# Three passes of the output projection cut anew (pairs 0-3 | query tiles 0-3 with pairs 4-5 | pairs 6-7 with tiles 4-7), passes that hold other tasks while they wait, and a shorter warm-up

## The chip, the cores and the metric

The kernel runs on one NeuronCore of one Trainium2 chip. The metric is the device time of one execution in microseconds, the median of a few runs. TensorE (PE) does the matrix products into PSUM, VectorE (DVE), ScalarE (ACT) and GpSimd (POOL) the rest of the arithmetic; SyncE (SP) issues most DMAs, ACT some. The instructions of each engine stand in one order, fixed when the program is built, and wait on semaphores for the other engines.

## What is computed

One trunk layer of a decoder for a prompt of 256 tokens and 8 single-token decode sequences (264 columns together): a half-step SwiGLU feed-forward, a mixing block in which half of the heads are sliding-window attention with sinks and half are an RWKV-7 recurrence, an output projection with residual, a second half-step feed-forward and a last normalisation.

```python
x = x + FFN_RES * swiglu(rmsnorm(x, n1), f1g, f1u, f1d)
h = rmsnorm(x, nm)
proj = h @ w_in
...
o_att, k_buf, v_buf = attend(q, k, v, sinks)
o_rwkv, shift, S = rwkv_time_mix(proj[..., ATT_COLS:], shift0, wkv0, mu, w0, w2, a0, a2, g2,
                                 k_k, k_a, r_k, ln_w, ln_b)
mixed = jnp.concatenate([o_att, o_rwkv.astype(o_att.dtype)], axis=-1)
x = x + mixed @ w_out
x = x + FFN_RES * swiglu(rmsnorm(x, n2), f2g, f2u, f2d)
...
y = rmsnorm(x, final_norm)
```

The model width is 2048, the feed-forward width 5504, the weights are float32.

## The kernel before

Activations stand transposed: 16 tiles of 128 features by 264 columns. Every large product is made from two-part operands: a weight tile and an activation are each split into a rounded part `hi` (type fp32r) and a remainder `lo`, and three matmuls of 264 columns (hi·hi, hi·lo, lo·hi) take the place of one. `chunk` (line 116) brings the weights: a DMA on SP's queue of up to four 128x128 blocks into `raw` (six buffers), a cast to `hi` on ACT (line 123), a subtraction to `lo` on DVE (line 124); `hi` and `lo` have four buffers each. `gemm` (line 127) runs the three matmuls per block (line 74 is the helper through which all matmuls go) into a PSUM tile `acc` (three buffers), and calls `step` after each chunk. The other PSUM tiles, `m`, have five buffers.

Three stages follow each other: `first_ffn`, `mixing`, `second_ffn`. In `mixing` the kernel is written as generators. The list `tasks` holds those that are under way, and `tick` (line 78) takes each of them one `yield` further. While the 38 tiles of the input projection are made by `win` (line 367), `tick` is the step of `gemm`, so that after each chunk every task issues its next piece. The tasks are: `prep` and `chain`, the recurrence of a batch of two pairs of heads (`bat[0]` to `bat[3]`, pairs 0-1, 2-3, 4-5, 6-7; the chain solves a triangular system on DVE, writes the result `Xt` to DRAM (`sb`, line 546) and reads it back into `TT` (line 551), both on SP's queue, and ends with a group norm, `gnorm`); `kvtask`; `attend`, the attention of one query tile over the prompt (eight tiles, named `o`); and `dec_attend(p)`, the decode attention of four tiles at once, which writes the last 8 columns of these tiles (line 824). `dec_load(p)` brings the cache for it.

The output projection (line 880 on) sums 16 tiles of `mixed`: entries 0 to 7 are the pairs of the recurrence (tiles `y`), 8 to 15 the query tiles (tiles `o`). It runs in passes, by the table

```python
PASS = [[0,1,2,3,8,9,10,11],[4,5,6,7],[12,13,14,15]]
```

A pass first calls `drain(need(ks))`: it ticks all tasks until the ones that made its inputs have ended. Then `split` (line 871) casts each input to `s` on ACT (line 873) and takes the remainder on POOL for even and on DVE for odd indices, and for each of the 16 outputs one `gemm` over the inputs of the pass follows, again with `tick` as step, and an addition on DVE into the residual (line 890). So the passes have 24, 12 and 12 matmuls an output. The rows of `w_out` are laid out by the same table (line 982).

The order on each engine is not the order of writing alone: the framework schedules the whole recorded program by a model of its timeline, with priority by the place in the program, and raises what stands under `tc.high_priority()` (the weights' chunks, the splits of a pass, the additions into the residual).

At the start of the program stands a warm-up of TensorE: POOL fills the constant tile `C` with ones, DVE casts it into a buffer of the ring `hi`, and 44 matmuls of 512 down to 128 columns run on it (lines 153 to 158), while the first inputs are loaded.

Of the kernel before, what the change touches and what calls it, by code (L numbers as in the profile page):

```python
# [8 lines left out]
F32R = mybir.dt.float32r  # L9
# [4 lines left out]
P = 128  # L14
# [13 lines left out]
CH, NRAW, NHL = 4, 6, 4  # L28
NACC, NM = 3, 5
NS, NO, NY, NH, NT, NLD = 38, 8, 8, 40, 18, 6  # L30
WARM = (512,) * 6 + (384,) * 6 + (264,) * 8 + (256,) * 8 + (192,) * 8 + (128,) * 8
NGM, NKR, NUV, NTT, NBT = 10, 5, 3, 2, 5
NSTEP = 4
DWAIT = (8,8,8,4)
# [2 lines left out]
LKV = 26  # L37
SEQ = [('b', 0), ('b', 1), ('b', 2), ('b', 3), ('kv', 0), ('kv', 1), ('kv', 2), ('kv', 3), ('q', 0), ('q', 1), ('q', 2), ('q', 3), ('q', 4), ('q', 5), ('q', 6), ('q', 7)]
NSO = (12, 13)
PASS = [[0,1,2,3,8,9,10,11],[4,5,6,7],[12,13,14,15]]  # L40

VG1, VGM, VG2, VGF = 0, 16, 32, 48
VMU, VKK, VKA, VA0, VRK, VLW, VLB, VSK, VSD = 64, 90, 98, 106, 114, 122, 130, 138, 154
# [4 lines left out]
def body(tc, I, O):  # L48
# [4 lines left out]
    def uid(s):  # L53
        cnt[0] += 1
        return f"{s}{cnt[0]}"
# [17 lines left out]
    def mm(out, lhsT, rhs, start=True, stop=True, **k):  # L73
        TE.matmul(out, lhsT, rhs, start=start, stop=stop, **k)  # L74

    tasks = []
# [6 lines left out]
    def drain(only, hold=()):  # L83
        while any(g in only for g in tasks):
            tick(hold)

    def spawn(g):
        tasks.append(g)
        return g
# [5 lines left out]
    with ExitStack() as ctx:  # L95
# [54 lines left out]
        G.memset(eps[:, 1:2], 64e-5)  # L150
        act(eps[:, 0:1], eps[:, 0:1], AF.Copy)

        G.memset(C, 1.0)
        wr = wp.tile([P, CH * P], F32R, tag="hi", bufs=NHL, name=uid("hi"))
        V.tensor_copy(wr, C[:, :CH * P])
        warm = mp()
        for n in WARM:
            mm(warm[:, :n], wr[:, :P], wr[:, :n])

        def vc(i):  # L160
            return vec[:, i:i + 1]
# [173 lines left out]
        def mixing_body(mx, n2, n3, XD):  # L335
# [351 lines left out]
            def kvtask(w, p, x):  # L687
                A.dma_start(O[("kp", "vp")[w]][p], x[:, P:NP])
                yield
                tp = mp()  # L690
                TE.transpose(tp[0:8, 256:384], x[:, NP:T], ident)
                if w:
                    for tb in range(2):
                        TE.transpose(tp[:, tb * P:(tb + 1) * P], x[:, tb * P:(tb + 1) * P], ident)
                    Vt[p] = slot((P, 2, P))
                    A.copy(Vt[p], tp[:, :256].rearrange("p (c t) -> p c t", c=2))
                if p == 0:
                    kvn[w] = tmp((8, 256))
                A.copy(kvn[w][:, p * P:(p + 1) * P], tp[0:8, 256:384])
                if p:  # L700
                    A.dma_start(O[("ks", "vs")[w]][:, 127, :], kvn[w])
                    if w:
                        A.dma_start(vnd, kvn[w])
                        while bat[-2] in tasks:
                            yield
                        dec_load(0)

            def softmax(s, mxv, sinks, n):
                nm, sm, es = (ring((P, 2), "st" + x, 6) for x in "abc")
# [51 lines left out]
            vnd = dp.tile([NB, 256], F32, tag="vnd", name="vnd")  # L761
            dk, dv, db, vr, qb = ([None] * 2 for _ in range(5))

            def dec_load(p):
                dk[p], dv[p] = ring((P, NB, P), "uv", NUV), ring((P, NB, P), "uv", NUV)
                dm = ring((P, 3, 256), "bk", 2)
                qb[p], vr[p], db[p] = (dm[:, i] for i in range(3))
                qb[p] = qb[p].rearrange("p (b x) -> p b x", b=NB)
                vr[p] = vr[p].rearrange("p (s x) -> p s x", s=2)
                db[p] = db[p][:, 0:129]  # L770
                SP.dma_start(dk[p], I["kc"][p])
                SP.dma_start(dv[p], I["cw"][p])
                SP.dma_start(db[p], I["bd"][p])
                G.memset(qb[p], 0.0)
                src = vnd.rearrange("(s g) d -> g s d", s=2)
                for g in range(4):
                    SP.dma_start(vr[p][g * 32:g * 32 + 32],
                                 bc(src[g:g + 1, :, p * P:(p + 1) * P], (32, 2, P)))

            def dec_attend(p, qs):  # L780
                for i, q in enumerate(qs):
                    for h in range(2):
                        G.tensor_copy(qb[p][HALF[h], :, h * 4 + i], q[HALF[h], NP:T])
                yield
                yield
                sps = mp()
                for b in range(NB):
                    g, x = b % 4 * 32, b // 4 * 129
                    mm(sps[g:g + 32, x:x + P], qb[p][:, b], dk[p][:, b])
                for b in range(NB):  # L790
                    g, x = b % 4 * 32, b // 4 * 129 + P
                    mm(sps[g:g + 32, x:x + 1], qb[p][:, b], kT[p][:, NP + b:NP + b + 1])
                dm = ring((P, 768), "bk", 2)
                s = dm[:, 0:258].rearrange("p (s x) -> p s x", s=2)
                pt = dm[:, 258:514].rearrange("p (s x) -> p s x", s=2)
                od = dm[:, 514:546].rearrange("p (i b) -> p i b", i=4)
                mxv = ring((P, 2), "mxv", 6)
                for j in range(2):
                    V.tensor_tensor_reduce(out=s[:, j], in0=sps[:, j * 129:j * 129 + 129], in1=db[p], op0=ALU.add,
                                           op1=ALU.max, scale=1.0, scalar=vc(VSD + p), accum_out=mxv[:, j:j + 1])  # L800
                softmax([s[:, 0], s[:, 1]], mxv, vc(VSD + p), 2)
                yield
                yield
                tp = mp()
                for j in range(2):
                    TE.transpose(tp[:, j * P:(j + 1) * P], s[:, j, 0:P], ident)
                A.copy(pt, tp[:, 0:2 * P].rearrange("p (s x) -> p s x", s=2))
                yield
                op = mp()
                for b in range(NB):  # L810
                    g, j = b % 4 * 32, b // 4
                    mm(op[g:g + 32, j * P:(j + 1) * P], pt[:, j, g:g + 32], dv[p][:, b])
                oa = tmp((P, 2, P))
                for j in range(2):
                    stt(oa[:, j], vr[p][:, j], s[:, j, P:P + 1], op[:, j * P:(j + 1) * P], ALU.mult, ALU.add)
                yield
                tq = mp()
                for j in range(2):
                    TE.transpose(tq[:, j * P:(j + 1) * P], oa[:, j], ident)
                tv = tq[:, :2 * P].rearrange("p (b x) -> p x b", b=NB)  # L820
                for h in range(2):
                    A.copy(od[HALF[h]], tv[HALF[h], h * 4:h * 4 + 4, :])
                for i, q in enumerate(qs):
                    G.tensor_copy(q[:, NP:T], od[:, i])
                if p == 0:
                    while bat[-1] in tasks:
                        yield
                    dec_load(1)

            shifted(0, la)  # L830
            act(tw[0:64, :], la[0:64, :], AF.Tanh)
# [3 lines left out]
            for kind, i in SEQ:  # L835
# [18 lines left out]
                else:  # L854
# [6 lines left out]
                    if i % 4 == 3:  # L861
                        p = i // 4
                        d = spawn(dec_attend(p, qs[4 * p:]))
                        for a in att[4 * p:]:
                            a.append(d)
            n2.xs = None
            xr = [slot() for _ in range(KD)]
            for o in range(KD):
# [10 lines left out]

            k0 = 0  # L880
            for pi, ks in enumerate(PASS):
                drain(need(ks))
                with tc.high_priority():
                    for k in ks:
                        split(k)
# [158 lines left out]
```

## Time and profile before

| what | value |
| --- | --- |
| time, median of 3 runs | 2030.97 us (2028.06 to 2032.6) |
| the profiled execution's own time | 2028.85 us |
| its span, first to last instruction | 2027.1 us, mean granted clock of TensorE 0.993 |
| TensorE matmul busy | 1990.2 us, 98% of the span |
| DVE, ACT, POOL busy | 1329.2, 1039.3, 243.0 us |
| data moved | 347.58 MB read, 10.22 MB written, 177 GB/s over the span |

A row of a timeline gives the start in us from the span's start, the duration in us, engine, line, operation, the tile written and the tiles read, how often it occurs there, and in brackets the idle time of the engine ahead of it with the instruction that ended it. A row of a windows table gives a stretch of time and in it the busy time and number of instructions of each engine, the granted clock as a share of full speed, the share of the DMA engines' time and GB/s. Matmuls overlap, so the time of one is read from the distance of starts or from a count in a window, not from its own duration. A matmul of plain float32 stands in the trace as two.

### The profile page before, as it was taken

Reading aid. Unit: us, or ns where it says so; the run is one execution under the profiler, and the core shown is the slowest. Engines: PE = TensorE matmul, PEld = TensorE weight load, DVE = VectorE, ACT = ScalarE, POOL = GpSimd, SP = SyncE. Lnnn points to the kernel's source line nnn. Section 1 sums busy time; section 2 is a strip of 40 time slices with the busy share of each in tenths; the row PEclk is TensorE's granted clock in tenths of the full one; section 3 lists DMA queues with packets and bytes.
Section 4 is the critical chain, followed back from the end, with each engine's and each line's share of the span. In section 5 each row is a group of like instructions: output and inputs, shape, how many; then the busy total and the mean of one; then the engine's idle time right before and its main releaser. Section 6 shows DMA issues by size and latency. Waiting matters only on the chain.

```text
span 2027.1 us, 45546 instructions
## 1 busy us (share of the span) xinstructions
PE 1990.2 (98%) x17142; PEld 1954.5 (96%) x17142; DVE 1329.2 (66%) x2659; ACT 1039.3 (51%) x2038; POOL 243.0 (12%) x343
## 2 busy tenths in 40 slices
PE   9999999999999999999897999999999999999998
PEld 9999999999999999999896799999999999999998
DVE  5865555655556577678777767775666666666665
ACT  5644444444444467665454654554444444444445
POOL 0401001010110122121110000120101101010012
PEclk9999999999999999999998999999999999999999
DMA  6566565655556566554455245565666565656654
GB/s 228 177 187 197 183 193 188 186 184 176 186 170 192 181 206 206 149 160 123 139 152 168 86 135 181 172 185 178 191 182 195 182 190 188 189 192 181 195 181 145
DMA packets 226493, 358.72 MB, mean 177 GB/s; under 512 B 42312, under 2 KB 79328, under 8 KB 226272
## 3 DMA queue, kind: packets, MB, share of 16 engines
q1 hardware_dynamic: 219808, 347.28, 55.0%
q10 hardware_dynamic: 6464, 8.54, 1.3%
q8 instruction: 134, 2.20, 0.4%
q14 instruction: 87, 0.71, 0.1%
HBM read 347.58 MB, written 10.22 MB: 177 GB/s over the span
## 4 chain that ended last, share of the span: by engine, by line
PE 90%; DVE 4%; DMA 3%; SPq 1%; issue 1%; ACT 1%; POOL 0%; DVEq 0%; ACTq 0%; POOLq 0%
PE acc L74 82%; PE m L74 7%; DVE lo L58 1%; DMA raw<-in_win 1%; DMA TT<-sb 1%; DMA sb<-Xt 0%; DVE t L680 0%; DVE st L58 0%; SPq L530 0%; DVE Xt L58 0%; DVE y L58 0%; ACT L68 0%; DMA Xt<-sa 0%; DMA raw<-in_wout 0%; ACT t L68 0%
## 5 line engine op out<-in xcount | busy, mean ns | idle before, releaser
L58 DVE TENSOR_TENSOR lo<-raw,hi 128x512 fp32r<-128x512 f32 (+1 forms) x1288 | 870.3, 679 | 539.1 <-ACT hi L123 515.5
L123 ACT CAST hi<-raw 128x512 fp32r<-128x512 f32 (+1 forms) x1288 | 777.0, 607 | 855.1 <-PE acc L74 776.3
L74 PE MATMUL acc<-s,hi 128*128 128x264 f32 x5940 | 1105.6, 286 | 7.4 <-ACT s L873 7.4
L74 PEld LDWEIGHTS acc<-s,hi 128*128 128x128 f32 x5940 | 922.7, 188 | 12.9 <-ACT s L873 8.2
L74 PE MATMUL acc<-s,lo 128*128 128x264 f32 x2970 | 846.8, 286 | 4.1 <-DVE lo L58 4.0
L74 PEld LDWEIGHTS acc<-s,lo 128*128 128x128 f32 x2970 | 559.0, 188 | 6.7 <-DVE lo L58 5.1
L74 PE MATMUL acc<-t,hi 128*128 128x264 f32 x2752 | 503.0, 284 | 0.0
L74 PEld LDWEIGHTS acc<-t,hi 128*128 128x128 f32 x2752 | 426.5, 188 | 0.0
L74 PE MATMUL acc<-t,lo 128*128 128x264 f32 x1376 | 389.1, 285 | 0.0
L58 POOL TENSOR_TENSOR t<-t,t 128x264 f32<-128x264 f32 (+1 forms) x148 | 151.1, 1021 | 1149.0 <-ACT hi L123 790.1
L74 PEld LDWEIGHTS acc<-t,lo 128*128 128x128 f32 x1376 | 258.5, 188 | 0.1
L74 PE MATMUL acc<-y,hi 128*128 128x264 f32 x648 | 124.1, 285 | 0.0
L74 PEld LDWEIGHTS acc<-y,hi 128*128 128x128 f32 x648 | 101.1, 188 | 0.2
L74 PE MATMUL acc<-y,lo 128*128 128x264 f32 x324 | 92.0, 284 | 0.0
L58 DVE TENSOR_TENSOR t<-acc,t 128x264 f32<-128x264 f32 x156 | 67.3, 432 | 35.8 <-PE acc L74 35.6
L58 POOL TENSOR_TENSOR o<-o,o 128x264 f32<-128x264 f32 x43 | 36.5, 850 | 229.8 <-ACT o L68 224.9
L74 PE MATMUL acc<-o,hi 128*128 128x264 f32 x324 | 62.6, 283 | 0.0
L74 PEld LDWEIGHTS acc<-y,lo 128*128 128x128 f32 x324 | 60.9, 188 | 0.0
L61 DVE SCALAR_TENSOR_TENSOR s<-acc,s 128x264 f32<-128x264 f32 x96 | 40.5, 427 | 16.0 <-PE acc L74 15.5
L74 PEld LDWEIGHTS acc<-o,hi 128*128 128x128 f32 x324 | 49.8, 188 | 0.0
L74 PE MATMUL m<-s,hi 128*128 128x264 f32 x260 | 47.8, 284 | 0.0
L61 DVE SCALAR_TENSOR_TENSOR x<-acc,x 128x264 f32<-128x264 f32 x96 | 40.4, 426 | 10.0 <-PE acc L74 9.6
(236 smaller groups left out, 1300.9 us busy)
## 6 DMA issues: line engine op xcount, KB each, us to landing
raw<-in_gu SPq DMA_DIRECT2D x688, 256.0 KB, 3.3
raw<-in_dn SPq DMA_DIRECT2D x224, 256.0 KB, 2.8
raw<-in_win SPq DMA_DIRECT2D x152, 256.0 KB, 3.5
raw<-in_dn SPq DMA_DIRECT2D x160, 192.0 KB, 2.8
raw<-in_wout SPq DMA_DIRECT2D x64, 256.0 KB, 3.2
xsp<-x ACTq DMA_DIRECT2D x16, 132.0 KB, 3.7
s<-xsp SPq DMA_DIRECT2D x16, 132.0 KB, 3.4
ld<-in_sT SPq DMA_DIRECT2D x16, 128.0 KB, 3.3
```

Of the source, the lines that this page charges most:

```text
L58: return e.tensor_tensor(out=out, in0=a, in1=b, op=op)
L61: return V.scalar_tensor_tensor(out=out, in0=a, scalar=s, in1=b, op0=op0, op1=op1)
L74: TE.matmul(out, lhsT, rhs, start=start, stop=stop, **k)
L123: A.copy(hi[:, :w], raw[:, :w])
```

## The change

Four things are edited.

1. The table `PASS` becomes `[[0,1,2,3],[8,9,10,11,4,5],[6,7,12,13,14,15]]`: 12, 18 and 18 matmuls an output. The chunks of a pass of six inputs are of four and of two blocks, so the projection has 80 chunks where it had 64, of the same bytes in all, and 80 ticks.
2. A pass that waits takes on only the tasks it needs: `drain(now, [g for g in tasks if g not in now])`.
3. `dec_load` becomes a task of its own that waits for the tasks whose buffers it takes over; `dec_attend` waits until its tiles are there. Before, `kvtask` and `dec_attend(0)` waited in its place.
4. The warm-up is 14 plain float32 matmuls of 128 columns on the tile `ones`; the fill of `C` and the cast are gone.

```diff
-WARM = (512,) * 6 + (384,) * 6 + (264,) * 8 + (256,) * 8 + (192,) * 8 + (128,) * 8
+NWARM = 14
...
-PASS = [[0,1,2,3,8,9,10,11],[4,5,6,7],[12,13,14,15]]
+PASS = [[0,1,2,3],[8,9,10,11,4,5],[6,7,12,13,14,15]]
...
-        G.memset(C, 1.0)
-        wr = wp.tile([P, CH * P], F32R, tag="hi", bufs=NHL, name=uid("hi"))
-        V.tensor_copy(wr, C[:, :CH * P])
         warm = mp()
-        for n in WARM:
-            mm(warm[:, :n], wr[:, :P], wr[:, :n])
+        for _ in range(NWARM):
+            mm(warm[:, :P], ones, ones)
...
                     if w:
                         A.dma_start(vnd, kvn[w])
-                        while bat[-2] in tasks:
-                            yield
-                        dec_load(0)
+                        spawn(dec_load(0, [bat[-2]]))
...
-            def dec_load(p):
+            def dec_load(p, after):
+                while any(g in tasks for g in after):
+                    yield
                 dk[p], dv[p] = ring((P, NB, P), "uv", NUV), ring((P, NB, P), "uv", NUV)
...
             def dec_attend(p, qs):
+                while dk[p] is None:
+                    yield
                 for i, q in enumerate(qs):
...
                     G.tensor_copy(q[:, NP:T], od[:, i])
-                if p == 0:
-                    while bat[-1] in tasks:
-                        yield
-                    dec_load(1)
...
                         for a in att[4 * p:]:
                             a.append(d)
+                        if p == 0:
+                            spawn(dec_load(1, [bat[-1], d]))
...
             for pi, ks in enumerate(PASS):
-                drain(need(ks))
+                now = need(ks)
+                drain(now, [g for g in tasks if g not in now])
```

**How the instructions stand, first place: TensorE after the last matmul of the input projection.** `m<-s,o` are attention scores, `m<-sgl,ld` the gate of pairs 4-5, `m<-C,t` transposes of softmax results; `acc<-s,...` right behind them are the first matmuls of the output projection. Before:

```order
L74 MATMUL acc_16335<-s_10584,lo_16450 128x264
L74 MATMUL m_15235<-s_14460,o_15157 128x256
L74 MATMUL m_15235<-s_14460,o_15157 128x128
L74 MATMUL m_15274<-sgl,ld_15133 128x264
L74 MATMUL m_15278<-sgl,ld_15135 128x264
L74 MATMUL acc_16538<-s_16506,hi_16540 128x264
L74 MATMUL acc_16618<-s_16506,hi_16620 128x264
L745 MATMUL m_15384<-C,t_15241 128x128
```

And now:

```order
L74 MATMUL acc_16302<-s_10551,lo_16417 128x264
L74 MATMUL m_15202<-s_14427,o_15124 128x256
L74 MATMUL m_15202<-s_14427,o_15124 128x128
L74 MATMUL m_15241<-sgl,ld_15100 128x264
L74 MATMUL m_15245<-sgl,ld_15102 128x264
L74 MATMUL acc_16489<-s_16473,hi_16491 128x264
L74 MATMUL acc_16521<-s_16473,hi_16523 128x264
L74 MATMUL acc_16571<-s_16473,hi_16573 128x264
L74 MATMUL acc_16489<-s_16474,hi_16491 128x264
L74 MATMUL acc_16489<-s_16473,lo_16492 128x264
```

Up to the second-solve products of pairs 6-7 (`m<-TT,zs`) 24 projection matmuls stood before, and 119 stand now; from there to the first product of the decode attention of tiles 0-3 (`m<-uv,bk`) 12 and 61; from there to the first matmul on a query tile none and 12. The attention and recurrence matmuls between them are the same.

**ScalarE at the same place.** `L123 CAST` are weight chunks, `L68 ACTIVATE t,stb` the exponentials of the softmax of query tile 4, `L873 CAST` (now `L870`) the splits of the first pass. Before:

```order
L68 ACTIVATE t_15143<-m_15217,eps 128x264
L123 CAST hi_16694<-raw_16693 128x512
L68 ACT_TABLE_LOAD
L68 ACTIVATE t_15240,stb_15246<-t_15240,sta_15245 128x256
L68 ACTIVATE t_15241,stb_15246<-t_15241,sta_15245 128x128
L68 ACTIVATE stc_15247<-sta_15245,vec 128x2
L68 ACTIVATE t_15292,stb_15298<-t_15292,sta_15297 128x256
L68 ACTIVATE t_15293,stb_15298<-t_15293,sta_15297 128x128
L68 ACTIVATE stc_15299<-sta_15297,vec 128x2
L873 CAST s_16506<-y_12725 128x264
L873 CAST s_16510<-y_12726 128x264
```

And now:

```order
L68 ACTIVATE t_15110<-m_15184,eps 128x264
L123 CAST hi_16649<-raw_16648 128x512
L870 CAST s_16473<-y_12692 128x264
L870 CAST s_16477<-y_12693 128x264
L870 CAST s_16481<-y_13753 128x264
L870 CAST s_16485<-y_13754 128x264
L68 ACT_TABLE_LOAD
L68 ACTIVATE t_15207,stb_15213<-t_15207,sta_15212 128x256
L68 ACTIVATE t_15208,stb_15213<-t_15208,sta_15212 128x128
```

The four splits stood behind both softmax halves of that tile and stand ahead of them now.

**Second place: VectorE where the read-back of the triangular solve of pairs 6-7 is used** (`TT<-TT,C`). `s<-acc,s` is the addition into the residual that frees a bank `acc`, `L736 ISA` (now `L731`) the softmax's maximum. Before, right behind the gate operations:

```order
L736 ISA t_15293,mxv_15294<-m_15235,ld_15192,vec 128x128
L736 ISA mxv_15294 128x1
L58 TENSOR_TENSOR y_14838<-m_15141,t_15143 128x264
L58 TENSOR_TENSOR TT_14729<-TT_14729,C 32x8x32
L65 TENSOR_SCALAR sta_15245<-mxv_15242 128x2
L58 TENSOR_TENSOR TT_14729<-TT_14729,C 32x8x32
```

And now, with the last step of the solve (`Xt`), which stood 16 rows ahead of that place, at its head:

```order
L58 TENSOR_TENSOR Xt_14687<-Xt_14687,st_15252 128x8
L710 RECIPROCAL stb_15213<-stb_15213 128x2
L58 TENSOR_TENSOR stb_15265<-stb_15265,stc_15266 128x2
L65 TENSOR_SCALAR t_15207<-t_15207,stb_15213 128x256
L65 TENSOR_SCALAR t_15208<-t_15208,stb_15213 128x128
```

```order
L731 ISA t_15366,mxv_15367<-m_15359,ld_15329,vec 128x128
L731 ISA mxv_15367 128x1
L58 TENSOR_TENSOR TT_14696<-TT_14696,C 32x8x32 x2
L745 COPY t_15404<-m_15399 128x128
L731 ISA t_15407,mxv_15409<-m_15360,ld_15331,vec 128x256
L731 ISA mxv_15409 128x1
L731 ISA t_15408,mxv_15409<-m_15360,ld_15331,vec 128x128
L731 ISA mxv_15409 128x1
L58 TENSOR_TENSOR s_16444<-acc_16647,s_16444 128x264
```

The solve ends later on DVE, its read-back is used later, and the addition for the fourth output of the first pass stands behind it.

**Third place: TensorE ahead of the first matmul on a query tile.** `m<-uv,bk` and `m<-C,bk` belong to the decode attention, `m<-y,C` and `m<-t,C` to the norm of pairs 6-7. Before:

```order
L74 MATMUL m_15927<-uv_15330,bk_15332 32x128 x8
L74 MATMUL m_15927<-s_14460,bk_15332 32x1 x8
L74 MATMUL m_15987<-y_15617,C 128x264
L74 MATMUL m_15991<-y_15618,C 128x264
L74 MATMUL m_15995<-t_15844,s_14815 64x256
L74 MATMUL m_15995<-t_15907,s_14815 64x256
L74 MATMUL m_15995<-t_15845,s_14815 64x128
L74 MATMUL m_15995<-t_15908,s_14815 64x128
L806 MATMUL m_16022<-C,bk_15944 128x128
```

And now, the last three of the twelve matmuls of the pass's last output being shown:

```order
L74 MATMUL acc_16940<-s_16485,hi_16942 128x264
L74 MATMUL acc_16940<-s_16486,hi_16942 128x264
L74 MATMUL acc_16940<-s_16485,lo_16943 128x264
L74 MATMUL m_15954<-y_15584,C 128x264
L74 MATMUL m_15958<-y_15585,C 128x264
L74 MATMUL m_15962<-t_15811,s_14782 64x256
L74 MATMUL m_15962<-t_15874,s_14782 64x256
L74 MATMUL m_15962<-t_15812,s_14782 64x128
L74 MATMUL m_15962<-t_15875,s_14782 64x128
L805 MATMUL m_15989<-C,bk_15911 128x128
```

Twelve projection matmuls came in between the decode attention's first product and the norm; from the norm on the rows are those of before, up to the first matmul on a query tile.

## The prediction

> **What bounds the kernel now.** I read the page first, then the busy times by stretches, then the timeline where TensorE is not full.
>
> ```profile
> PE 1990.2 (98%) x17142; PEld 1954.5 (96%) x17142; DVE 1329.2 (66%) x2659; ACT 1039.3 (51%) x2038; POOL 243.0 (12%) x343
> PE 90%; DVE 4%; DMA 3%; SPq 1%; issue 1%; ACT 1%; POOL 0%; DVEq 0%; ACTq 0%; POOLq 0%
> L74 PE MATMUL acc<-s,hi 128*128 128x264 f32 x5940 | 1105.6, 286 | 7.4 <-ACT s L873 7.4
> ...
> 1050.00:1100.00 50.00, 48.19 (x583) 43.68 (x582) 38.58 (x123) 23.81 (x53) 2.86 (x7) 1.00 0.61 172
> 1100.00:1150.00 50.00, 36.69 (x437) 28.60 (x436) 36.40 (x138) 25.91 (x86) 3.65 (x11) 0.82 0.37 107
> 1150.00:1200.00 50.00, 50.00 (x393) 42.45 (x393) 35.20 (x119) 28.24 (x86) 3.93 (x11) 0.98 0.38 113
> 1200.00:1250.00 50.00, 50.00 (x414) 50.00 (x413) 38.91 (x72) 25.01 (x44) 2.23 (x4) 1.00 0.52 178
> ```
>
> TensorE sets the end. The fifty us from 1100 are the exception: 36.7 us busy at a clock of 0.82. That is the wait of the first output pass, which the table edits. The last row gives the price of a projection matmul, which all counts below use: 50 us / 414 = 0.1208 us.
>
> The hole in front, engine by engine (PE, ACT, DVE, SP):
>
> ```profile
> 1097.16 0.92 PE L74 MATMUL m<-s,o 64*128 64x256 f32 x4
> 1099.47 0.71 PE L74 MATMUL m<-sgl,ld 128*128 128x264 f32 x2 [0.75 <-DVE mxv L736]
> 1107.59 0.81 PE L74 MATMUL acc<-s,hi 128*128 128x264 f32 x2 [7.41 <-ACT s L873]
> 1109.52 0.47 PE L745 MATMUL m<-C,t 128*128 128x128 f32 x1 [1.12 <-DVE t L65]
> ...
> 1097.15 0.62 ACT L123 CAST hi<-raw 128x512 fp32r<-128x512 f32 x1 [1.51 <-PE acc L74]
> 1103.94 0.51 ACT L68 ACTIVATE t<-t,sta 128x256 f32<-128x256 f32 x1 [4.87 <-DVE sta L65]
> 1107.14 1.33 ACT L873 CAST s<-y 128x264 fp32r<-128x264 f32 x4
> ...
> 1093.79 0.17 DVE L58 TENSOR_TENSOR Xt<-Xt,st 128x8 f32<-128x8 f32 x1
> 1101.28 0.43 DVE L58 TENSOR_TENSOR y<-m,t 128x264 f32<-128x264 f32 x1
> 1103.41 0.41 DVE L58 TENSOR_TENSOR TT<-TT,C 32x256 f32<-32x256 f32 x1 [1.69 <-DMA TT<-sb]
> 1104.38 0.49 DVE L61 SCALAR_TENSOR_TENSOR y<-y,vec,t 128x264 f32<-128x264 f32 x1
> ...
> 1094.82 3.56 SPq L546 DMA_DIRECT2D sb<-Xt  x4
> ```
>
> DVE waits for `TT`, behind it stand the maxima for the softmax, behind these ACT's exponentials, behind these the casts of the splits: TensorE loses 7.41 us. From the solve's end (1093.79) to `TT` (1103.41) pass 9.6 us of DRAM round trip.
>
> The second hole, and the clock:
>
> ```profile
> 1120.13 0.69 PE L74 MATMUL m<-TT,zs 32*32 32x32 f32 x30
> 1134.83 0.65 PE L74 MATMUL m<-uv,bk 128*32 128x128 f32 x16
> 1140.45 0.33 PE L806 MATMUL m<-C,bk 128*128 128x128 f32 x1 [2.99 <-DVE bk L65]
> 1145.44 1.53 PE L74 MATMUL m<-s,o 64*128 64x256 f32 x4 [1.45 <-DVE t L750]
> 1151.60 0.99 PE L74 MATMUL acc<-s,hi 128*128 128x264 f32 x3
> ...
> 1112.00:1114.00 2.00, 2.00 (x12) 2.00 (x10) 0.93 (x5) 0.96 (x5) 0.00 (x0) 0.50 0.04 11
> 1148.00:1150.00 2.00, 2.00 (x8) 1.38 (x6) 1.34 (x5) 1.24 (x6) 0.77 (x4) 0.50 0.29 76
> ...
> 916.97 0.48 PE L74 MATMUL m<-BT,W 64*64 64x64 f32 x4 [1.96 <-DVE uv L598]
> 917.00:919.00 2.00, 2.00 (x34) 1.88 (x36) 1.86 (x6) 0.32 (x1) 0.00 (x0) 0.50 0.18 58
> 919.00:921.00 2.00, 2.00 (x54) 2.00 (x52) 2.00 (x5) 0.00 (x0) 0.00 (x0) 0.67 0.01 4
> ```
>
> After each hole the granted clock is 0.50. A wait of 1.96 us is enough for it at 917, and the 0.50 lasts there for some 3.4 us (2 us and two thirds of the next two): about 1.7 us lost each time.
>
> **The passes and the held tasks.** The order in the text above gives three landmarks on PE: A, the second-solve products (1120.13); B, the decode attention's first product (1134.83); C, the first matmul on a query tile (1151.60). At C the old program has done 36 of 768 projection matmuls, the new one 192; what follows C needs the same attention work and 156 matmuls less: 156 x 0.1208 = 18.8 us gained, if C came at the same time. C comes later, by what the inserted matmuls take and the waits leave:
>
> - *To A*: 95 matmuls more, 11.5 us, so 1131.6 with the old waits. The splits now stand ahead of the exponentials on ACT and can run at 1097.8, so the 7.41 us wait and the half clock after it go. New waits, walking down the new order: the second input's remainder is on DVE behind the `y` of 1101.28 and four operations of up to 0.49 us, at about 1103.0, while PE has 12 matmuls (1.45 us) from 1100.2 (1099.47 + 0.71): 1.3 us. Then, the late read-back: the solve's last step now stands on DVE behind some ten such operations of the gate and the softmax, about 1105.3 instead of 1093.8; 8.6 us later (from 1094.82, when SP began to write, to 1103.41) `TT` is there, 1113.9. Behind it stands the addition that frees a bank for the seventh output; with the maxima in between it ends at about 1116.2. PE has six outputs (8.7 us) and 3 to 4 us of attention (four scores in 0.92 us) until 1113.9: 2.3 us. The second half of `TT` costs some 2 us more, the transposes 0.3. Sum 5.9, where the old program lost 7.41 + 1.12 + half of the 7.4 us at half clock from 1107.6 to 1115, 12.2 in all. So 6.3 us are won and A is at **1125.3**. Bounds: none of the new waits, 1119.4; all of the old loss in the new places, 1131.6.
> - *A to B*: 14.7 us as before, and 49 matmuls, 5.9: **B 1145.9**. DVE gets 0.69 + 0.43 us for each output more,
>
> ```profile
> L58 DVE TENSOR_TENSOR lo<-raw,hi 128x512 fp32r<-128x512 f32 x66 | 45.5, 693 | 12.5 <-ACT hi L123 8.4 <-issue 0.3
> L58 DVE TENSOR_TENSOR s<-acc,s 128x264 f32<-128x264 f32 x48 | 20.6, 431 | 12.0 <-PE acc L74 11.7
> ```
>
>  below the 1.45 us that PE takes for one, so these hide behind it; without that cover each output would cost up to 1.1 us more.
> - *B to C*: 16.8 us before. Twelve matmuls (1.45 us) go into the wait of 2.99; the addition and one `lo` of the same output (0.8) stand ahead of the decode softmax on DVE: 17.6, **C 1163.5**. The tail itself is not touched, it keeps its waits and half clock (bounds: 3.4 less at full clock, 2 more).
>
> Net: 18.8 - (1163.5 - 1151.6) = **6.9 us won**.
>
> The 16 added chunks carry no bytes and stand under full passes after C: nothing; without cover 16 x 0.69 = 11 us at most. The last pass needs pairs 6-7 and tiles 4-7, which were long there before; the decode result of these tiles goes ahead of 42 matmuls (5.1 us) now, and from its last transpose to its write (PE, POOL)
>
> ```profile
> 1197.66 0.33 PE L819 MATMUL m<-C,t 128*128 128x128 f32 x1
> 1199.63 0.57 POOL L824 COPY o<-bk 128x8 f32<-128x8 f32 x4
> ```
>
>  the trace has 2.5 us: hidden, 0; if the splits queue, up to 4. Holding tasks and `dec_load` as a task move rows by a few places in the input projection: 0, bounds 2 either way.
>
> **The warm-up.**
>
> ```profile
> 1.61 0.43 DVE L155 CAST hi<-C 128x512 fp32r<-128x512 f32 x1 [1.61 <-POOL C L153]
> 2.09 7.91 PE L74 MATMUL m<-hi 128*128 128x512 f32 x44 [2.09 <-DVE hi L155]
> 9.84 0.46 PE L74 MATMUL acc<-s,hi 128*128 128x264 f32 x2
> 7.63 1.64 ACT L123 CAST hi<-raw 128x512 fp32r<-128x512 f32 x3
> 8.27 1.90 DVE L58 TENSOR_TENSOR lo<-raw,hi 128x512 fp32r<-128x512 f32 x3
> ...
> 2016.05 1.36 PE L74 MATMUL m<-o,ones 128*128 128x128 f32 x10
> ```
>
> The old warm-up runs until the first real matmul at 9.84, though the first `hi` is there at 8.25. The new one is 28 half-products (the last row: 0.11 us each at full clock, twice that at half), from about 1 to 4 to 7 us. Real work can start at 8.3, 1.5 earlier, but runs at the pace of DVE's remainders until about 11. Then it is all but level with before, and PE has idled about 2 us and been half idle until then: by the row of 917 one to two stretches of half clock, 1.7 to 3.4 us. I take **1.5 us lost**, bounds 1.5 won and 3 lost.
>
> [...]
>
> **Sum.** 6.9 - 1.5 = 5.4 us less than the profiled execution's span of 2027.1 (own time 2028.85, 2.1 below the median 2030.97): span 2021.7, median 2025.6.
>
> **The rivals.**
>
> - [...] 0.10.
> - *The waits close*: `TT` arrives before it is needed and PE runs through (A at 1119.4, tail at full clock, start 0): 6.9 + 5.9 + 3.4 = 16.2 less, 2014.8. For it: PE has 119 matmuls to lay over it. Against: the order on DVE. 0.10.
> - *The wait only moves*: A at 1131.6. 0.6 won and 1.5 lost: 2031.9. It happens when `TT` is late by 6 us more, for instance because SP's queue, where the weight DMAs and the residual's 16 loads stand, issues the write late. 0.17.
> - [...] 0.15.
> - That the change doesn't do what it says is out: the order shows it.
>
> **How the numbers follow.** The forecast has 0.48; its own range is 2020 to 2030, by the bounds on A and the start. A measurement tells 0.2% (4 us, below 2026.9 or above 2035.0) from no change. Faster: 0.36 of the forecast and both first rivals, 0.56. Same: 0.12 of the forecast and 0.14 of the moved wait, 0.26. Slower: the clock and the rest of the moved wait, 0.18. The range leaves out the lower half of the closed waits and the upper part of the clock's: 2014 to 2037.
>
> **What would show it.** Right: no wait of PE for ACT's splits near 1100; `TT<-TT,C` about ten us later than 1103; A near 1125, C near 1163 with both its waits; the first real matmul near 8.3 with long distances until 12. Wrong: A after 1129, half clock across several stretches there, a new wait ahead of the last pass (the splits of tiles 4-7), or the input projection ending off 1097 by more than the start explains.

## The result, and the profile after

| | before, us | changed, us | ratio, 95% interval |
|---|---|---|---|
| first comparison, 12 and 12 runs | 2028.16 (2025.49 to 2032.60) | 2028.22 (2027.16 to 2029.30) | 0.9997 [0.9988, 1.0006] |
| second comparison, 27 and 11 runs | 2030.71 (2026.74 to 2034.35) | 2026.22 (2023.20 to 2029.32) | 0.9979 [0.9970, 0.9988] |
| profiled execution, own time / span | 2028.85 / 2027.1 | 2027.84 / 2026.1; second: span 2024.3 | |

No measurable difference at first, 0.2% faster in the repetition, in intervals that touch at their bounds: -1.2 to 2.4 us gained by the first, 2.4 to 6.1 by the second. The forecast was 5.4.

The page, the stretches and PE's timeline of the changed kernel (in the stretches: us, then busy us and instructions of PE, PEld, DVE, ACT and POOL, then the granted clock; in the timeline: start, duration, what ran, and in brackets the wait ahead of it and its cause):

```profile
PE 1994.1 (98%) x17126; PEld 1956.0 (97%) x17126; DVE 1324.4 (65%) x2674; ACT 1041.4 (51%) x2054; POOL 240.8 (12%) x342
PE 94%; DVE 2%; DMA 2%; ACT 1%; SPq 1%; issue 1%; ACTq 0%; DVEq 0%
L74 PE MATMUL acc<-s,hi 128*128 128x264 f32 x5940 | 1107.3, 286 | 3.9 <-DVE s L58 1.6
```

```profile
1100.00:1150.00 50.00, 46.51 (x556) 39.85 (x554) 41.42 (x151) 26.92 (x81) 1.44 (x2) 1.00 0.53 161
1150.00:1200.00 50.00, 44.45 (x300) 35.14 (x301) 35.17 (x127) 27.20 (x85) 5.63 (x17) 0.86 0.27 78
1200.00:1250.00 50.00, 50.00 (x414) 48.35 (x414) 33.43 (x80) 28.63 (x67) 2.17 (x6) 1.00 0.50 161
```

```profile
1099.74 1.35 ACT L870 CAST s<-y 128x264 fp32r<-128x264 f32 x4
1101.11 1.28 ACT L68 ACT_TABLE_LOAD   x1
...
1101.64 0.71 PE L74 MATMUL m<-sgl,ld 128*128 128x264 f32 x2 [0.85 <-DVE mxv L731]
1104.92 0.39 PE L74 MATMUL acc<-s,hi 128*128 128x264 f32 x1 [1.03 <-DVE s L58]
1112.55 0.41 DVE L58 TENSOR_TENSOR TT<-TT,C 32x256 f32<-32x256 f32 x1 [0.82 <-DMA TT<-sb]
1119.25 0.49 PE L74 MATMUL acc<-s,hi 128*128 128x264 f32 x2 [0.61 <-DVE s L58]
1124.48 0.69 PE L74 MATMUL m<-TT,zs 32*32 32x32 f32 x32
1144.91 0.53 PE L74 MATMUL m<-uv,bk 128*32 128x128 f32 x12
1152.21 0.33 PE L805 MATMUL m<-C,bk 128*128 128x128 f32 x1 [3.21 <-DVE bk L65]
1157.20 0.66 PE L74 MATMUL m<-s,o 64*128 64x256 f32 x1 [1.45 <-DVE t L745]
1165.08 1.42 PE L74 MATMUL acc<-s,hi 128*128 128x264 f32 x3 [1.24 <-ACT s L870]
```

The 7.4 us wait of the first splits is gone: ACT casts all four `s` at 1099.74, ahead of the exponentials. The fifty us from 1100 are nearly full at full clock; the hole now lies behind B (1144.91), in the fifty us from 1150, which before were full. From 1200 on nothing waits.

Stretch by stretch (from starts of matmuls in the traces; "control" and "again" are second executions of the same rows, e4 and e12 below):

| us | before / control | changed / again | table alone / same rows (e1, e3) | warm-up alone (e2) |
|---|---|---|---|---|
| start to the projection's first matmul | 763.63 / 763.73 | 763.72 / 764.16 | 763.97 / 763.66 | 763.60 |
| input projection | 333.32 / 334.12 | 335.30 / 333.57 | 334.77 / 333.38 | 336.17 |
| its last matmul to the second FFN | 161.37 / 160.75 | 156.65 / 156.20 | 153.55 / 153.79 | 166.10 |
| of this, lost: up to A | 12.8 / 12.3 | 5.1 / 5.6 | 12.4 / 12.7 | 10.8 |
| of this, lost: A to B | -0.3 / -0.3 | -2.0 / -2.0 | -2.0 / -2.0 | 5.4 |
| of this, lost: from B on | 12.9 / 12.9 | 17.7 / 16.7 | 7.2 / 7.2 | 14.0 |
| second FFN, first to last matmul | 755.92 / 755.95 | 757.38 / 757.38 | 756.64 / 756.64 | 755.06 |

"Lost" is the length of a stretch less its matmuls, each at the median distance of its kind from its start to the next one's; idle time and half clock both land there. A is the first product of the second solve; in the kernel before, two of the 32 run at 1118.63, ahead of the other thirty at 1120.13. The first profile's sum, changed less before: 0.1 + 2.0 - 4.7 + 1.5 = -1.1 us, and the spans differ by 1.0.

### The profile page after: what moved, and what is told of

It reads as the page before. It is cut to its first block, busy times and chain, and to the rows that moved or that the text cites. A ratio compares the mean times of both kernels' runs of the same rounds, so it can differ in the third digit from the quotient of the medians.

```text
span 2026.1 us, 45592 instructions
## 1 busy us (share of the span) xinstructions
PE 1994.1 (98%) x17126; PEld 1956.0 (97%) x17126; DVE 1324.4 (65%) x2674; ACT 1041.4 (51%) x2054; POOL 240.8 (12%) x342
## 4 chain that ended last, share of the span: by engine, by line
PE 94%; DVE 2%; DMA 2%; ACT 1%; SPq 1%; issue 1%; ACTq 0%; DVEq 0%
PE acc L74 85%; PE m L74 8%; DVE lo L58 1%; DMA TT<-sb 0%; DMA sb<-Xt 0%; DVE y L58 0%; DMA raw<-in_gu 0%; DMA ld<-in_sT 0%; DVE st L58 0%; SPq L122 0%; DVE Xt L58 0%; ACT t L68 0%; DVE uv L595 0%; DMA Xt<-sa 0%; PE m L495 0%
## 5 line engine op out<-in xcount | busy, mean ns | idle before, releaser
L58 DVE TENSOR_TENSOR lo<-raw,hi 128x512 fp32r<-128x512 f32 (+2 forms) x1304 | 871.8, 673 | 552.5 <-ACT hi L123 526.5
L123 ACT CAST hi<-raw 128x512 fp32r<-128x512 f32 (+2 forms) x1304 | 779.3, 602 | 861.6 <-PE acc L74 776.3
```

What stands on the lines that cost most here:

```text
L58: return e.tensor_tensor(out=out, in0=a, in1=b, op=op)
L123: A.copy(hi[:, :w], raw[:, :w])
```

## The experiments

**One part alone (e1 to e4).** Four kernels between the two:

```diff
 e1: before with
-PASS = [[0,1,2,3,8,9,10,11],[4,5,6,7],[12,13,14,15]]
+PASS = [[0,1,2,3],[8,9,10,11,4,5],[6,7,12,13,14,15]]
 e2: before with
-        for n in WARM:
-            mm(warm[:, :n], wr[:, :P], wr[:, :n])
+        for _ in range(NWARM):
+            mm(warm[:, :P], ones, ones)
 (and without the fill of C and the cast)
 e3: changed, with the old warm-up, its fill and its cast put back
 e4: before with
-                drain(need(ks))
+                now = need(ks)
+                drain(now, [g for g in tasks if g not in now])
 and dec_load as a task
```

> The kernel before with the new table of passes alone (old warm-up, old draining, old place of the decode load). Theory: the whole gain of the passes comes from the table, so the stretch from the end of the input projection to the first matmul of the second FFN is 4.7 us shorter than before, as in the changed kernel, the input projection ends where it did before (within 0.3 us), and the median is 4 to 5 us under the kernel before, about 2023.5. Rival 1: the gain needs the held tasks; then the second-solve products come at about 1131.6 and at most 0.6 us are won, about 2027.6. Rival 2: the second FFN is slower by 1.4 us because of the new passes (other slots or queues in it); then its mean distance of matmuls is 122.0 ns, not 121.75, and the median is about 2025.

Measured: 2023.63 us, ratio 0.9974 [0.9964, 0.9985], 5.1 us under the 2028.71 of before beside it. The passes are 7.8 us shorter, more than expected, and the second FFN's mean distance is 121.88 ns, between theory and rival 2. Rival 1 is out: the gain needs no held task. But it lies elsewhere than in the changed kernel, from B on.

> The kernel before with the new, short warm-up alone. Theory: the 2.07 us that the input projection lost in the changed kernel come from this edit, since it alone changes the order of the rows between 800 and 1100 us; the first real matmul is at 8.3, the first FFN is level with before from about its 100th matmul, the projection ends 2.07 us later, nothing else changes, and the median is about 2 us above the kernel before, 2030.2. Rival 1: the 2.07 us come from the held tasks and the decode load; then this kernel is level with before from 20 us to the end, 2028.2. Rival 2 (the prediction's term): the start itself loses 1.5 us; then the first FFN ends 1.5 us late.

Measured: 2035.18 us, 1.0033 [1.0021, 1.0044]: slower by 6.5. The start is level, against rival 2, and the projection 2.9 us longer; but the larger loss, 4.7 us, is in the passes, where the theory had none.

> The changed kernel with the old warm-up put back. Theory: it has the gain of the passes without the loss in the input projection: 4.7 us from the end of the projection to the second FFN, and no loss ahead, so about 2023.5, better than both kernels, and the same as the new table alone. Rival: the 2.07 us belong to the held tasks; then this kernel ends where the changed kernel does, 2028, and differs from the table alone by 2 us.

Measured: 2023.95 us, 0.9974 [0.9965, 0.9984], as e1; below the changed kernel's 0.9997, while its second interval, from 0.9970 on, overlaps. The traces have it 2.4 to 2.9 us ahead in the passes and 0.7 in the second FFN. Compared row by row, e1 and e3 issue the same instructions in the same order on all five engines.

> The kernel before with the held tasks and the decode load as a task, but the old table of passes and the old warm-up. Theory: with the old table these two edits move no row, so every landmark is within 0.2 us of before and the median 2028.2; the second FFN's mean distance of matmuls then shows how far two executions of the same rows differ. Rival: they are worth something by themselves, a gain or loss of 1 us or more, seen between 1040 and 1155 us.

Measured: 2029.55 us, 1.0002 [0.9993, 1.0011], and again the same rows as before: holding tasks and spawning `dec_load` change nothing, with either table. It is a control: passes within 0.6 us, second FFN within 0.03, projection 0.8 apart.

What moves rows between 800 and 1260 us is thus the table and the warm-up at the start. That holding and spawning move nothing agrees with a scheduler that sorts the rows by a timeline of its own; that the warm-up's length shifts this is seen in e10 and e11, where only the count of its products differs. PE, ACT and the 6 us stretches of the table with the old warm-up (e3):

```profile
1107.37 1.03 PE L74 MATMUL acc<-s,hi 128*128 128x264 f32 x3 [7.09 <-ACT s L873]
...
1154.00:1160.00 6.00, 5.78 (x47) 4.52 (x47) 6.00 (x12) 1.58 (x4) 0.37 (x2) 1.00 0.11 36
1160.00:1166.00 6.00, 3.89 (x25) 2.44 (x22) 4.33 (x20) 4.17 (x12) 3.28 (x13) 1.00 0.58 162
1166.00:1172.00 6.00, 5.83 (x41) 4.74 (x42) 5.41 (x17) 4.93 (x17) 2.31 (x3) 1.00 0.06 21
```

and what PE waited for from 1097 to 1260 in the new warm-up with the old table (e2; total, times, longest):

```profile
PE m L74 <- DVE stb L712: 3.6, 1, 3.6
PE m L74 <- DVE TN L558: 2.3, 1, 2.3
PE acc L74 <- ACT s L870: 2.2, 1, 2.2
```

With the table and the old warm-up the wait in front stays (7.09 for ACT's splits), but 93 of the 192 matmuls of the first pass are left at B, and the clock reads 1.00 through the tail, 1154 to 1172. With the new warm-up the splits come early, 180 are used up by B, and the tail is bare, with the clock at 0.78, 0.50 and 0.58 in the same three stretches. With the new warm-up and the old table the first splits come early too (from 1100.5), but only 36 matmuls stand ready: two new waits just ahead of A (3.6 and 2.3) and one behind B for the splits of the query tiles (2.2).

**Filling the place behind B (e5 to e8).** Pairs 4-5 are ready at 1106 (their last `y`), and can be a pass of their own; and the splits of pairs 0-3 can be issued by a task of their own, ahead of query tile 7 (EARLY is 6):

```diff
 e5: changed, e6: e3, each with
-PASS = [[0,1,2,3],[8,9,10,11,4,5],[6,7,12,13,14,15]]
+PASS = [[0,1,2,3],[4,5],[8,9,10,11],[6,7,12,13,14,15]]
 e7: e3, e8: e6, each with
+            def early():
+                while any(g in tasks for g in bat[:2]):
+                    yield
+                with tc.high_priority():
+                    for k in PASS[0]:
+                        split(k)
...
+                    if i == EARLY:
+                        es = spawn(early())
...
+                if pi == 0:
+                    now = [es]
...
+                if pi:    # the splits of the later passes alone
```

> The changed kernel with a fourth pass: pairs 4-5 (whose y is ready at 1106) as a pass of their own after pairs 0-3, then query tiles 0-3, then pairs 6-7 with tiles 4-7. Theory: the changed kernel closes the hole in front by spending nearly all of its 192 matmuls there (180 are done when the decode attention begins, and 12 are left for the waits behind it), so the waits of 3.2, 1.5 and 1.2 us and the half clock come back behind it; 96 more matmuls (11.6 us) that need no query tile fill that place. Lost time from the decode attention's first product to the second FFN falls from 17.7 us to 8 to 11, the median from 2028.2 to about 2020. Rival: the waits there are latencies of DVE's chain, which the passes' own additions and splits lengthen, so that the end comes no earlier; then within 2 us of the changed kernel.

Measured: 2019.61 us, 0.9953 [0.9940, 0.9965]. Lost from B on 9.1 us, not 17.7; passes 147.6 us. The theory holds. (The changed kernel's ratios to the same kernel before are 0.9997 and 0.9979.)

> The same four passes with the old warm-up, where the hole in front stays (the casts of the first splits stand behind the exponentials on ACT) and 93 matmuls are still left at the decode attention. Theory: the place behind it is already nearly filled there (7.2 us lost), so the 96 matmuls more bring at most 3 us: 2021 to 2024; the front still loses 12 to 13 us. Rival: the additional matmuls are worth as much here as with the new warm-up, 7 us: 2017.

Measured: 2023.87 us, 0.9971 [0.9959, 0.9982], level with e3; 12.8 us lost in front, 7.1 from B on. So 96 more matmuls are worth 9 us of the passes where the place is bare and nothing where it is filled.

> The three passes of the change with the old warm-up, and the splits of pairs 0-3 issued as soon as their pairs are done, two query tiles earlier, so that their casts stand ahead of the exponentials on ACT; the input projection keeps its order. Theory: matmuls that need no query tile are a fixed amount, 192; by its order this kernel has them all done when the decode attention begins, so what the front gains (lost time 12.7 to about 4 us) the place behind loses (7.2 to about 17), and the time is 2022 to 2026, level with the old warm-up without it (2023.9). Rival: the two holes are independent; then it gains 8 us and is at 2016.

Measured: 2019.17 us, 0.9952 [0.9940, 0.9965]: 4.7 us under e6 beside it (which is level with e3), between theory and rival. Not all of it is the passes: in the profiled executions they are 2.6 us shorter than in e6 and the second FFN 2.0 shorter (755.13, not 757.17), which neither has a term for, while the projection is 2.0 longer. In front 3.6 us are lost, as expected; from B on 12.7, not 17, with no matmul of the first pass left. Its tail has the first two waits of the changed kernel's, not the third, and more clock: 0.85 and 0.87 in the stretches from 1154 and 1160.

```profile
1152.81 0.33 PE L809 MATMUL m<-C,bk 128*128 128x128 f32 x1 [3.00 <-DVE bk L66]
1157.80 1.29 PE L75 MATMUL m<-s,o 64*128 64x256 f32 x4 [1.44 <-DVE t L749]
...
1154.00:1160.00 6.00, 4.38 (x31) 3.07 (x30) 5.86 (x14) 2.39 (x5) 1.41 (x6) 0.85 0.06 17
1160.00:1166.00 6.00, 6.00 (x32) 4.38 (x31) 4.90 (x22) 4.62 (x19) 2.95 (x10) 0.87 0.38 108
```

> Early splits and four passes together, with the old warm-up: 288 matmuls that need no query tile, 120 of them in front. Theory: both holes are filled, lost time about 4 in front and 8 to 11 behind: 5 to 8 us under the three passes with the old warm-up, 2016 to 2019, the fastest of all. Rival: DVE, which is busy for 17 to 21 of each 25 us there, becomes the bound with 16 additions and splits more; then 2022 or more.

Measured: 2021.59 us, 0.9961 [0.9948, 0.9973]: slower than expected. In front 3.3 us are lost, but from B on 12.2: 229 of the 288 matmuls are used up by B, and 59 are left, where e5 keeps 108. Two waits stand behind B, one for ACT and one for DVE; that the smaller stock causes them is argued from the counts, and the rival is not excluded:

```profile
1161.09 0.33 PE L744 MATMUL m<-C,t 128*128 128x128 f32 x1 [2.03 <-ACT t L69]
1164.73 1.65 PE L75 MATMUL m<-s,o 64*128 64x256 f32 x4 [1.43 <-DVE t L749]
```

e5 and e7 are the fastest versions, about 10 us under the kernel before; their intervals do not tell them apart, and e8's overlaps both.

**What was left over (e9 to e12).** The projection's 2 us, the second FFN's pace, and whether the order alone decides the passes:

```diff
 e9: changed with
-NSO = (12, 13)
+NSO = (8, 9)
 e10: e3 with
-WARM = (512,) * 6 + (384,) * 6 + (264,) * 8 + (256,) * 8 + (192,) * 8 + (128,) * 8
+WARM = (512,) * 6
 e11: e3 with (128,) * 16 at the end of WARM
 e12: changed, as it is
```

> The changed kernel, but tiles 8 and 9 of the second FFN's input (not 12 and 13) go into the ring o; up to the end of the passes nothing is moved. Theory: the second FFN's pace depends on the slots in which its moving tiles lie, since in the kernels so far the matmuls on t tiles agree (121.81 to 121.88 ns) and those on s, o and y tiles do not; so here its mean distance leaves 122.000 by 0.1 ns or more (0.6 us over 6191 matmuls), in either direction, and t tiles stay at 121.8 to 121.9. Rival: the pace is set ahead of the second FFN (by what runs or lies there since the passes); then 122.00 within 0.02.

Measured: 2027.74 us, 0.9986 [0.9977, 0.9995]; mean distance 122.02 ns (757.51 us from first to last matmul, 757.38 in the changed kernel). The theory falls. The kinds of tiles shifted against each other (start to next start, without the few longer than 200 ns: `acc<-o,hi` 121.4 to 123.4, `acc<-y,hi` 121.8 to 120.4) and the mean stayed within 0.02: the slots of these tiles do not give the pace. That something set before the second FFN does is what is left, and not shown.

> The three passes, the held tasks and the old warm-up cut to its six products of 512 columns. The scheduler then gives the rows of the input projection and of the passes the changed kernel's order. Theory: what the new warm-up cost is that order (2 us in the projection, 3 in the passes against the old warm-up), not its products; so this kernel is at 2027 to 2029 as the changed one is, with the projection 336 us long, not 334, and 20 to 21 us lost in the passes. Rival: the order is without effect, the new products at the start cost it; then it is at 2024 as with the old warm-up.

Measured: 2030.64 us, 0.9997 [0.9988, 1.0005]. From 26 us on, this kernel is row for row the changed one, as said. Its time is above even the theory's range, but not by what the theory names: the projection begins at 766.25 us (763.72 and 764.16 in the changed kernel) and takes 339.5, more than either expected, and the passes take 154.4, with 18.5 us lost, less than expected and only 0.6 more than e3. e9, whose rows up to the second FFN are the changed kernel's too, has passes of 155.3. So one order gave 156.7, 156.2, 155.3 and 154.4 us in four executions: what it costs there against e3 is 0.6 to 2.9 us, not a fixed 3.

> The three passes with the old warm-up made longer by eight products of 128 columns (0.9 us). The scheduler makes a third order of it for the projection, and in the passes it spends 180 of the 192 matmuls ahead of the decode attention, as in the changed kernel. Theory: which order the start leads to decides, and the passes' order decides most: 19 to 21 us lost in the passes, as in the changed kernel, so 2025 to 2029. Rival: a longer warm-up is what is good for the passes; then 18 us or less lost there, 2024 or less.

Measured: 2022.87 us, 0.9961 [0.9947, 0.9974]; the projection 333.5 us, the passes 152.8 with 16.9 lost. The theory fails here: by its order all but 12 matmuls are gone at B, as in the changed kernel, and the tail still costs 14.6 us, not 17.7. With e7, which has none left and loses 12.7, this shows that the count left at B does not set the tail's loss alone; what else does is open.

> The changed kernel once more, for how far two executions of the same rows differ. Theory: start and order are fixed, so the projection takes 335 to 337 us, the passes lose 20 to 21.5 us with about 5 in front and 17 to 18 behind, the second FFN's mean distance is 122.00; median 2028. Rival: these differences are chance; then one of them leaves its range.

Measured: 2026.22 us, 0.9979 [0.9970, 0.9988]. Passes 156.2 and second FFN 122.00 ns as in the first execution; the projection 333.57, out of its range. So its 2 us are not settled: the new rows took 333.2 (e9), 333.6, 335.3, 336.2 (e2), 337.1 (e5) and 339.5 us (e10), 335.8 in the mean; the old ones 333.3 to 334.8 in five executions, 333.9 in the mean, and with a few rows moved 335.7 (e7) and 333.2 (e8). A part may belong to the order, but two of the six show none of it; what makes them spread stays open.

What differs between executions of one order in the tail is the clock, and behind the first wait (3.21 us in both) also the next two (1.45 and 1.24 us, then 0.96 and 1.86). The 6 us stretches behind B, the changed kernel first, then again (e12):

```profile
1154.00:1160.00 6.00, 4.40 (x28) 3.22 (x28) 5.98 (x15) 0.52 (x2) 1.63 (x7) 0.78 0.07 17
1160.00:1166.00 6.00, 4.28 (x18) 2.49 (x17) 2.98 (x12) 4.43 (x13) 1.81 (x8) 0.50 0.37 107
1166.00:1172.00 6.00, 6.00 (x30) 5.27 (x31) 3.85 (x16) 3.97 (x17) 2.20 (x3) 0.58 0.00 0
```

```profile
1154.00:1160.00 6.00, 5.04 (x33) 3.51 (x32) 6.00 (x15) 0.82 (x3) 1.79 (x8) 0.78 0.08 20
1160.00:1166.00 6.00, 3.37 (x20) 2.36 (x19) 3.19 (x13) 5.41 (x18) 1.64 (x7) 0.78 0.37 104
1166.00:1172.00 6.00, 6.00 (x38) 4.82 (x38) 4.13 (x17) 4.15 (x15) 2.21 (x3) 0.81 0.00 0
```

## Why the prediction was right or wrong

The time lies in the range that was given, by the range's width and not by the sum: 5.4 us did not come, the profiles' spans give 1.0 and 2.8. Of the difference, 2.2 (in the second execution 1.7) are in the passes, 2.0 (0.3) in the projection and 1.5 in the second FFN, and 1.4 (1.0) came back at the start. Neither the closed nor the moved wait is what happened: A came at 1124.5 (not 1119 or 1131). The clock stayed at 1.00 from 1100 to 1150 and fell behind B, to 0.86 in the fifty us from 1150. Step by step:

- *To A*: the walk of the waits was right in kind, they are smaller, and the place was met in part by luck. `TT` came at 1112.55 (forecast 1113.9). PE idled 1.03 and 0.61 us at places that were walked and 0.85 at one that was there before: 2.5 in all, at a clock of 1.00, where 5.9 were forecast (the table's measure, against distances, says 5.1). A came at 1124.48, again at 1123.70 (1125.3), but the projection had ended 2.1 and 0.8 us later than before: from its end A took 25.5 and 26.0 us, not 28.4. The cause was put down to the table; e1 and e3 show that the table leaves the wait (7.09) and that the warm-up's edit, by its order, removes it.
- *A to B*: right, B at 1144.91 and 1144.13 (1145.9).
- *B to C*: **the step that failed**, by its wait. Forecast 17.6 us: twelve matmuls (1.45 us) were to go into the wait of 2.99, 0.8 us of DVE work to stand ahead of it, so that about 2.3 of it are left. Measured 20.2 and 20.0 (C at 1165.08 and 1164.11). The wait did not shrink, it is 3.21; and two waits were not in the walk, 0.46 us for ACT and 1.24 (again 1.86) for the casts of the query tiles' splits. PE idles 6.5 us from B to C in both executions, 4.6 before. The half clock, kept in the forecast, is the old one here: 0.81 and 0.83, before 0.82 (the stretch from B to C, then the one behind C; before, changed, again):

```profile
1134.83:1151.60 16.77, 12.15 (x98) 8.42 (x94) 13.50 (x51) 10.82 (x34) 3.02 (x14) 0.82 0.26 80
1151.60:1158.00 6.40, 6.40 (x48) 5.76 (x47) 4.73 (x17) 4.36 (x17) 2.04 (x3) 0.94 0.07 23
...
1144.91:1165.08 20.17, 13.64 (x107) 9.58 (x106) 13.93 (x50) 11.01 (x36) 2.69 (x13) 0.81 0.29 92
1165.08:1172.00 6.92, 6.89 (x32) 5.86 (x33) 4.74 (x17) 4.89 (x19) 2.94 (x4) 0.57 0.00 0
...
1144.13:1164.11 19.98, 13.48 (x108) 9.83 (x107) 13.85 (x50) 11.11 (x36) 2.69 (x13) 0.83 0.31 93
1164.11:1172.00 7.89, 7.58 (x43) 6.19 (x44) 5.54 (x21) 6.04 (x22) 2.95 (x4) 0.78 0.00 1
```

 Why the wait did not shrink stands on DVE and ACT. It ends 7.30 us after B, before 5.62: not 0.8 later but 1.68, more than the 1.45 that the matmuls fill. The maxima (`sta`) on DVE start 3.64 us after B, before 2.52, which is 1.12 later; the exponentials behind them 4.40, before 2.72, which is 1.68 later. The other 0.56 is on ACT: the copy `o<-m` stood behind the exponentials, stands ahead of them now, and waits 0.42 us for a product that PE has behind the twelve matmuls. Before, then now:

```profile
1137.35 0.29 DVE L65 TENSOR_SCALAR sta<-mxv 128x2 f32<-128x2 f32 x2
1137.55 0.51 ACT L68 ACTIVATE t<-t,sta 128x256 f32<-128x256 f32 x1 [0.47 <-DVE sta L65]
1139.59 0.35 ACT L758 COPY o<-m 128x256 f32<-128x256 f32 x1
...
1148.55 0.23 DVE L65 TENSOR_SCALAR sta<-mxv 128x2 f32<-128x2 f32 x2
1149.05 0.37 ACT L753 COPY o<-m 128x256 f32<-128x256 f32 x1 [0.42 <-PE m L74]
1149.31 0.51 ACT L68 ACTIVATE t<-t,sta 128x256 f32<-128x256 f32 x1
```

 That e5 brings the loss from B on from 17.7 to 9.1 by laying 96 matmuls there shows that the place lacked work.

- *After C, 156 matmuls less, 18.8 us*: the count is right. From C to the second FFN the kernel before takes 106.7 us and e3, whose clock reads 1.00 there, 87.8: 18.9. In the changed kernel it is 90.6 and 89.8, 2.7 and 1.9 us more than the forecast's 87.9: the half clock reaches past C, where the granted clock is 0.57 and 0.78 until 1172, and was 0.94 behind the old C. The forecast had no term for that.
- *Net 6.9 in the passes*: 4.7 and 5.2. With the table alone it would have been 7.6 to 7.8, for another reason.
- *The warm-up, 1.5 lost*: wrong, 0.1 and 0.5. The forecast of the start was right (first real matmul at 8.27, longer distances until 11.5), that the half clock would come back after it was not: from 9.0 on distances of 0.12 us stand between single longer ones, and from the 52nd real matmul on the kernel is level with before within 0.1 us.
- *Input projection, 0 within 2*: 2.0 and 0.3, at the bound and inside. That holding tasks and `dec_load` move its rows was wrong (e4); the warm-up moves them.
- *The added chunks and the last pass at 0*: right, no wait from 1200 on.
- *The second FFN*: no term, and 1.5 us lost in both executions, to the hundredth.

The price of a gap in clock was read from one row, 1.7 us after a wait of 1.96. The runs show no fixed price, and none shows from which length of wait on the clock falls. In the kernel before it reads 1.00 from 1136 to 1144, across the wait of 2.99 us, and 0.50 from 1146 to 1152, behind the next one (1.45); in the changed kernel 1.00 from 1148 to 1154, across the wait of 3.21 us, and 0.50 from 1158 to 1171, again behind the next one (1.45). The two fences of 6 us stretches above, of the same rows, differ: 0.78, 0.50, 0.58 in one execution and 0.78, 0.78, 0.81 in the other, behind the same wait of some 3.2 us.

## What to carry to other kernels

Matmuls that wait for nothing are a stock: count how many are left at each later hole, for those spent in front of one hole are missing behind it, and an edit that closes the first can open the second (180 of 192 used, and the tail lost 14.6 to 17.7 us instead of 7.2). And work laid into a wait can move the chain that ends it, on every engine of that chain: here 1.45 us of matmuls and what came with them moved the end by 1.68 us. Where a scheduler sorts the rows, an edit at the start is an edit everywhere: compare the rows of each part alone before a gain is put down to it. And keep second executions of the same rows beside a difference of 0.1%: here two of them gave the passes to 0.6 us and four only to 2.3, the second FFN to 0.03, and six the projection only to 6.

## What the runs showed of the hardware

The first products of the new warm-up, in the changed kernel, and the clock that the profile gives for them:

```profile
0.99 6.28 PE L74 MATMUL m<-ones 128*128 128x128 f32 x28 [0.99 <-POOL eps L150]
8.27 1.03 PE L74 MATMUL acc<-s,hi 128*128 128x264 f32 x4 [1.00 <-ACT hi L123]
...
0.00:4.00 4.00, 3.01 (x14) 3.01 (x15) 0.00 (x0) 1.49 (x2) 0.48 (x7) 1.00 0.45 101
```

All 28 run 0.213 us apart but for the first distance, 6.28 us without a pause. In e12, the same rows again, the distance falls to 0.111 at 4.35 us, 3.4 us after the first product, and in e2 at 6.65, 5.7 us after it; yet the clock reads 1.00 throughout. In these starts the column does not tell the slower pace (0.213) from the faster one (0.111); distances do. The first real matmuls do not tell the two apart: they stand 0.225 to 0.295 us apart until 9.0, and in e2 0.226 to 0.289, where the products before them ran at 0.111 already. The old warm-up's distances halve 3.4 us after its first product in the profile before and 5.9 us after it in e7, and the first real matmul follows at 9.84 and 10.92: with the same warm-up these two starts differ by 1.1 us.

PE's rows in the second FFN are the same in these kernels but for its first few, and its pace differs by kernel and repeats where the same rows were executed again. PE in the 500 us from 1300 (matmuls in brackets): before, control (e4), changed, again (e12), e3, e2:

```profile
1300.00:1800.00 500.00, 500.00 (x4112) 499.15 (x4111) 327.24 (x561) 242.84 (x431) 58.97 (x61) 1.00 0.60 186
```

```profile
1300.00:1800.00 500.00, 500.00 (x4111) 499.11 (x4110) 327.57 (x561) 243.10 (x431) 58.24 (x61) 1.00 0.59 186
```

```profile
1300.00:1800.00 500.00, 500.00 (x4105) 499.22 (x4104) 326.57 (x558) 241.85 (x429) 58.26 (x61) 1.00 0.59 185
```

```profile
1300.00:1800.00 500.00, 500.00 (x4104) 499.21 (x4104) 325.32 (x558) 241.28 (x426) 57.92 (x60) 1.00 0.62 185
```

```profile
1300.00:1800.00 500.00, 500.00 (x4109) 499.19 (x4108) 325.29 (x559) 241.03 (x424) 57.28 (x60) 1.00 0.60 186
```

```profile
1300.00:1800.00 500.00, 500.00 (x4117) 499.11 (x4116) 327.66 (x562) 243.30 (x431) 56.50 (x59) 1.00 0.60 186
```

Between the slowest and the fastest lie 13 matmuls in 4110, 0.3%, 2.3 us over the FFN, at a clock of 1.00 throughout. e9 excludes the slots of the tiles it moved; the cause stays open.
